# Score products over 64 rows stacked over 128 partitions, and rotated queries transposed two pieces later, in a two-layer encoder kernel

## The chip, the core and the metric

The kernel runs on one core of a Trainium2 chip. The metric is the device time of one execution, in microseconds (us). Before the change it is 834.36 us (median of 3 runs, 832.62 to 834.82).

The core has five engines that work side by side and wait for each other by semaphores: TensorE (PE; its weight loads are shown as PEld) multiplies matrices, VectorE (DVE), ScalarE (ACT) and GpSimd (POOL) work on elements, SyncE (SP) issues the transfers of the weights. TensorE writes to PSUM, and the other operands lie in SBUF; both have 128 partitions ("rows" of an operand below).

## The reference

An encoder trunk of two layers over 256 tokens of 2048 features, in float32. Each layer normalizes x, multiplies it with one wide input matrix, and hands the columns to three attention mixers whose gated results go through an output matrix and are added to x.

```python
for l in range(DEPTH):                      # 2
    h = rmsnorm(x, norm_g[l])
    (a_q, a_k, a_v, a_g, b_cq, b_ckv, b_kr, b_g,
     c_q, c_k, c_v, c_g) = split(h @ w_in[l])
    ya = swa_attention(...)    # A: 8 heads of 128, 2 key/value heads, window, sink
    yb = mla_attention(...)    # B: 4 heads
    yc = diff_attention(...)   # C: 4 heads
    x = x + concat(ya * silu(a_g), yb * silu(b_g), yc * silu(c_g)) @ w_out[l]
return rmsnorm(x, final_norm)

# B, scores of a head: 128 features of its own, and 64 rotated by the position
q_rope = rope(q[..., 128:], positions);  k_r = rope(k_rope, positions)
sc = (q_nope @ k_nope.T + q_rope @ k_r.T) * scale       # k_r is shared by the heads
# C, a head has two softmax maps over 64 features each
sc = (q[:, c] @ k[:, c].T) * scale - slope * dist       # c = 0, 1
attn = softmax(sc[0]) - lam * softmax(sc[1])
```

Two kinds of products run over 64 features: the rotated part of B's scores, and both maps of C.

## The kernel before, in words

*Split products.* A float32 operand x is kept as x = x1 + x2, two parts of 12 bits in the type fp32r. `halves` makes x1 on ScalarE (a copy that rounds) and x2 = x - x1 on VectorE. A full product is three matrix products, x1 y1, x1 y2, x2 y1 (`mm3`, lines 288 to 290).

*Pieces.* All weights come as a list of 266 pieces of up to 512 KB, in the order of use. For each, SP loads it (line 148, four buffers), ScalarE makes its high half `whi` (line 155) and VectorE, in some pieces GpSimd, its low half `wlo` (line 158); both halves have three buffers. The split runs two pieces ahead of the products. `proj_t` (lines 382, 383) uses a piece of four times 128 rows by 256 columns in 16 products; the up-projections of B use theirs in 12 to 24.

*Order.* The program is one long list: a piece's products, then whatever small tasks are due. `later(n, fn)` makes a task due n pieces on, and its first TensorE instruction keeps its place in TensorE's queue. A planner orders the rest within each engine; each engine runs its own queue strictly in order.

*Stacked products.* For 64 features, `stack_q` and `stack_k` put the two parts of an operand into the two halves of the 128 partitions. A pair of products gives the score: [q1; q1] with [k1; k2] over 128 rows (line 431), then q2 with k1 over 64 rows (line 432). `own(c)` is the half of the partitions in which part c lies. The helpers serve three users: `evac_c` (queries and keys of C, out of `proj_t`), `key_transpose` (the rotated key of B), and `finish` in `up_projections` (the rotated queries of B: `use_qr` makes them from a piece, GpSimd rotates them in `rope`, lines 653 to 658, and `finish` transposes them, line 696, three pieces after).

*Users of the scores.* `head_b` has per token tile three full products and one stacked pair, into one PSUM tile. `head_c` has for each map and token tile one stacked pair. The queries' stacked tiles lie in `keep` buffers (the tags yhi and ylo, which the results of the heads take later); `lo64` is a ring of four buffers.

Of the kernel before, what the change touches and what calls it, by code (L numbers as in the profile page):

```python
# [12 lines left out]
F32 = mybir.dt.float32  # L13
F32R = mybir.dt.float32r
# [5 lines left out]
P = 128  # L20
# [10 lines left out]
# 10000 ** (-2 i / 64) in float32  # L31
# [11 lines left out]
def turn_parts():  # L43
    """1 / (2 pi) cut into five parts of 12 bits, the first bit at 2**-3."""
    digits = 0x28BE60DB9391054A7F09D5F47D4D377036D8A5664F10E4107F9458EAF7AEF1586
    bits = 4 * len(f"{digits:x}")
    out, rest = [], digits
    for n in range(5):
        at = bits - 2 - 12 * (n + 1)
        out.append(math.ldexp(rest >> at, at - bits))  # L50
        rest &= (1 << at) - 1
    return out
# [3 lines left out]
def trunk(ctx, tc, x, positions, norm_g, w_in, swa_sink, mla_q_norm, mla_w_uq, mla_kv_norm, mla_w_ukv,  # L56
# [12 lines left out]
    @contextmanager  # L69
    def in_order(*engines, chain=False):  # L70
        """The first instruction that the block traces on each of these engines keeps its place behind
        those traced before it; with chain, all of them do."""
        engines = engines or (nc.tensor,)
        kinds = [e.engine for e in engines]
        traced = nc.cur_bb.bb.instructions
        n = len(traced)
        yield
        for kind in kinds:
            prev = next((i for i in reversed(traced[:n]) if i.engine == kind), None)
            for i in traced[n:]:  # L80
                if i.engine != kind:
                    continue
                if prev is not None:
                    tc.add_manual_dep(i, prev.name, mybir.DependencyInfo(
                        mybir.DependencyClass.NoSync, mybir.DependencyReason.DATA), reason="in_order")
                prev = i
                if not chain:
                    break
# [61 lines left out]
    def split(n):  # L150
        p = pieces[n]
        p["hi"] = wts.tile([P] + p["shape"], F32R, tag="whi", bufs=3, name=f"whi{n}")
        p["lo"] = wts.tile([P] + p["shape"], F32R, tag="wlo", bufs=3, name=f"wlo{n}")
        raw = p.pop("raw")
        nc.scalar.activation(p["hi"], raw, AF.Copy)  # L155
        # GpSimd takes a few of the differences, where VectorE has the attention to do as well
        eng = nc.gpsimd if n > 30 and n % 16 == 15 else nc.vector
        eng.tensor_tensor(p["lo"], raw, p["hi"].bitcast(F32), ALU.subtract)  # L158

    def halves(hi, lo, src, scale=1.0):  # L160
        """hi, lo <- scale * src (SBUF or PSUM) as two parts of 12 bits."""
        nc.scalar.activation(hi, src, AF.Copy, scale=scale)
        if scale == 1.0:
            nc.vector.tensor_tensor(lo, src, hi.bitcast(F32), ALU.subtract)
        else:
            nc.vector.scalar_tensor_tensor(lo, src, scale, hi.bitcast(F32), ALU.mult, ALU.subtract)

# [26 lines left out]
    def rope_constants():  # L194
        H = RD // 2
        # angles in turns, reduced exactly: position * inv is cut into two parts, 1/(2 pi) into five,
        # whose products are exact and lose their whole turns each
# [35 lines left out]
    def distance_constants():  # L233
        # |position - position|, from its upper and lower 16 bits, rounded once
# [17 lines left out]
    def lambdas():  # L252
        # lambda of the differential heads
        pr = work.tile([P, DEPTH, 2, 64], F32, tag="gate", bufs=4, name="lam_pr")
        nc.gpsimd.tensor_tensor(pr, lamp[:, :, :, 0, :], lamp[:, :, :, 1, :], ALU.mult)
        ls = small.tile([P, DEPTH, 2], F32, tag="ls", bufs=1, name="ls")
        later(16, lambda: nc.vector.tensor_reduce(ls, pr, AX.X, ALU.add), nc.vector)
        later(18, lambda: lambda_exp(ls), nc.scalar)
# [6 lines left out]
    def rsqrt(ss, n, w, name, base=None):  # L265
        """(ss / n + eps) ** -0.5 on [P, w]: exp and ln, then a step of Newton's. base: in eps's place."""
# [28 lines left out]
    def later(n, fn, *engines):  # L295
        """fn, n pieces from now; its first instruction on TensorE and on these engines keeps its place."""
        tasks.append((clock[0] + n, fn, engines))
# [10 lines left out]
    def x_stats(L, j, ts=range(NT)):  # L308
        """Sum of squares of one chunk of x, and its transpose times g, in two parts."""
        if not hasattr(L, "ss"):  # L310
            L.ss = small.tile([P, NT, 4], F32, tag="ss_x", bufs=2, name=f"ss{L.l}")
        for t in ts:
            junk = work.tile([P, 512], F32, tag="sb", bufs=3, name=f"sqx{L.l}_{j}_{t}")
            nc.scalar.activation(junk, xc[j][:, t, :], AF.Square, accum_out=L.ss[:, t, j:j + 1])
# [20 lines left out]
    def x_scale(L):  # L335
        """r = rsqrt(mean(x^2) + eps), as a column; x_scale_row: as a row over all partitions."""
        tot = small.tile([P, NT], F32, tag="ss_t", name=f"sst{L.l}")
        nc.vector.tensor_reduce(tot, L.ss, AX.X, ALU.add)
        L.r = rsqrt(tot, D, NT, f"rx{L.l}")
# [11 lines left out]
    def proj_a(L, w, c0, n, nkt, evac):  # L351
        """[token, feature] = h @ w[:, c0:c0+n]."""
# [17 lines left out]
    def proj_t(L, w, c0, evac):  # L370
        """[feature, token] of 256 columns; the two small products share their half of the bank."""
# [19 lines left out]
    def gather(L, f, ps):  # L391
        """f <- the two halves of ps added, times the norm's row."""
# [13 lines left out]
    # Products over 64 rows use both halves of the partitions: [q1; q1] with [k1; k2], and q2 with k1,  # L406
    # where x = x1 + x2. Part c keeps its own rows for x1 of the keys and for x2 of the queries.
# [3 lines left out]
    def stack_q(src, tags, name, scale=1.0):  # L411
        """src(c): the rows of part c. -> {c: [q1; q1]} and q2."""
        top = {}
        lo = work.tile([P, S], F32R, tag="lo64", bufs=4, name=f"lo{name}")
        for c, tag in enumerate(tags):
            t = top[c] = keep.tile([P, S], F32R, tag=tag, name=f"top{name}_{c}")
            for at in (c, 1 - c):
                nc.scalar.activation(t[own(at)], src(c), AF.Copy, scale=scale)
            nc.vector.scalar_tensor_tensor(lo[own(c)], src(c), scale, t[own(c)].bitcast(F32), ALU.mult, ALU.subtract)
        return top, lo  # L420

    def stack_k(src, tiles):
        """src(c): the rows of part c, in their own place. -> {c: [k1; k2]}, k1 in its own place."""
        for c, t in enumerate(tiles):
            nc.scalar.activation(t[own(c)], src(c), AF.Copy)
            nc.vector.tensor_tensor(t[own(1 - c)], src(c), t[own(c)].bitcast(F32), ALU.subtract)
        return dict(enumerate(tiles))

    def mm_stacked(ps, q, k, c, ts, first, last):
        top, lo = q  # L430
        nc.tensor.matmul(ps, top[c][:, ts], k[c], start=first, stop=False)  # L431
        nc.tensor.matmul(ps, lo[own(c), ts], k[c][own(c)], start=False, stop=last)  # L432

    def evac_c(L, dst, i, ps, scale, tag):
# [5 lines left out]
        else:  # L440
            dst[i] = stack_k(src, [keep.tile([P, S], F32R, tag=f"ylo{2 * i + c}", name=f"ck{L.l}_{i}_{c}") for c in range(2)])

    def evac_gate(L, dst, i, ps):
        """silu(g) = g / (1 + exp(-g)) = g exp(min(g, 0) - ln(1 + exp(-|g|)))"""
# [26 lines left out]
    def softmax(S_ps, sb, w, name):  # L471
        """sb[:, :, :w] <- exp(sb - max) in place (from S_ps if given); returns 1 / sum."""
# [67 lines left out]
    def head_b(L, h):  # L540
# [3 lines left out]
        def scores():  # L544
            ps = att.tile([P, NT, S], F32, tag="att", name=f"S{name}")
            (qh, ql), (kh, kl) = L.qb.pop(h), L.kb.pop(h)
            for t in range(NT):
                ts = slice(t * P, (t + 1) * P)
                mm3(ps[:, t, :], qh[:, ts], ql[:, ts], kh, kl, True, False)
                mm_stacked(ps[:, t, :], L.qr[h // 2], L.kr, h % 2, ts, False, True)  # L550
# [17 lines left out]
    def head_c(L, h):  # L568
# [3 lines left out]
        def scores():  # L572
            q, k = L.qc.pop(h), L.kc.pop(h)
            sbs, rrs = [], []
            for c in range(2):
                ps = att.tile([P, NT, S], F32, tag="att", name=f"S{name}_{c}")
                for t in range(NT):
                    mm_stacked(ps[:, t, :], q, k, c, slice(t * P, (t + 1) * P), True, True)
# [67 lines left out]
    def rope(dst, src, t, heads, tmp, name):  # L646
        """dst <- src turned by the angles of its tokens; [P, heads, 64] each."""
# [20 lines left out]
    def key_transpose(L, kt):  # L668
# [3 lines left out]
        L.kr = stack_k(lambda c: ps[own(c)], [work.tile([P, S], F32R, tag=f"kr{c}", bufs=1, name=f"kr{L.l}_{c}") for c in range(2)])  # L672

    def up_projections(L):
# [5 lines left out]
        def use_qr(p):  # L680
# [18 lines left out]
            later(3, finish)  # L699
# [66 lines left out]
    def out_chunk(L, j):  # L766
# [5 lines left out]
        # the columns of each token tile, per bank  # L772
# [53 lines left out]
    def final_add(L, j, t, ps, c):  # L826
        """x += ps in the columns c of chunk j, its sum of squares, and the gain; after the last ones the
        scale and the store."""
# [151 lines left out]
```

## Time and profile before

| | |
|---|---|
| median of 3 runs | 834.36 us |
| span of the profiled execution | 831.4 us; no time of its own is recorded beside it |
| TensorE / VectorE / ScalarE / GpSimd busy | 98 / 71 / 60 / 28% of the span |
| mean busy share of the 16 DMA engines | 58% |
| TensorE's mean granted clock | 0.997 of full speed |

A row of the page's costliest groups, of the list of groups and of one line's instructions names the line, the engine, the operation, what it writes and reads (output <- inputs, buffer numbers left out), the shape, and how often. TensorE's products overlap: a product's duration holds the time in which it passes through the array, while the next one has started. What a product takes of the engine is the distance between two starts.

### The profile page before, as it was taken

What the parts mean: (1) busy time and instruction counts of PE and PEld (TensorE: products, weight loads), DVE (VectorE), ACT (ScalarE), POOL (GpSimd) and SP (SyncE); (2) the same over time, 40 slices, a digit from 0 to 9 for tenths busy, and PEclk for the clock granted to TensorE, in tenths of its full rate; (3) what the DMA queues carried; (4) which work ended last, traced back from release to release, by engine and by line L of the source; (5) the groups of instructions that cost most, each with busy time, mean ns of one, the idle gap of its engine ahead of it and who ended that gap; (6) DMA issues with size and microseconds to landing.
All of it is one profiled execution on the core that took longest, in us unless ns stands there. A gap on an engine that the chain in (4) does not pass through costs nothing. (4 is left out here: it accounts for less than half of the span.)

```text
span 831.4 us, 12804 instructions
## 1 busy us (share of the span) xinstructions
PE 814.6 (98%) x4638; PEld 711.4 (86%) x4638; DVE 587.9 (71%) x951; ACT 495.2 (60%) x942; POOL 230.2 (28%) x266
## 2 busy tenths in 40 slices
PE   8999999999999999999999999999999999999996
PEld 7988888888988888888899888888889888888885
DVE  4767967879768787645556577779787877875554
ACT  5776666667556565554556465757665655664443
POOL 7234232213023444110001243311221432343210
PEclk9999999999999999999999999999999999999998
DMA  8666645464566465556557765464646565557652
GB/s 274 170 194 176 178 130 149 132 176 135 170 177 175 125 180 175 156 178 196 164 158 211 192 169 157 127 176 130 176 127 174 157 177 155 176 152 225 199 183 102
DMA packets 120415, 139.95 MB, mean 168 GB/s; under 512 B 8052, under 2 KB 97728, under 8 KB 120352
## 3 DMA queue, kind: packets, MB, share of 16 engines
q1 hardware_dynamic: 119712, 137.66, 57.2%
q0 software_dynamic: 640, 1.47, 0.6%
q8 instruction: 36, 0.59, 0.3%
q14 instruction: 27, 0.22, 0.1%
HBM read 137.02 MB, written 2.10 MB: 167 GB/s over the span
## 5 line engine op out<-in xcount | busy, mean ns | idle before, releaser
L158 DVE TENSOR_TENSOR wlo<-raw,whi 128x1024 fp32r<-128x1024 f32 (+2 forms) x250 | 297.4, 1194 | 161.7 <-ACT whi L155 160.1
L155 ACT ACTIVATE whi<-raw 128x1024 fp32r<-128x1024 f32 (+2 forms) x266 | 270.8, 1021 | 225.0 <-PE pt L382 78.0
L382 PE MATMUL pt<-h,whi 128*128 128x512 f32 x1088 | 390.0, 400 | 0.0
L383 PE MATMUL pt<-h,wlo 128*128 128x256 f32 x1088 | 305.2, 281 | 1.0 <-DVE wlo L158 1.0
L382 PEld LDWEIGHTS pt<-h,whi 128*128 128x128 f32 x1088 | 204.3, 188 | 46.8
L383 PEld LDWEIGHTS pt<-h,wlo 128*128 128x128 f32 x1088 | 205.6, 189 | 1.6 <-DVE wlo L158 1.6
L288 PE MATMUL po<-whi,yhi 128*128 128x512 f32 (+1 forms) x272 | 103.2, 379 | 0.0
L289 PE MATMUL po<-wlo,yhi 128*128 128x512 f32 (+1 forms) x272 | 102.6, 377 | 0.0
L290 PE MATMUL po<-whi,ylo 128*128 128x512 f32 (+1 forms) x272 | 102.6, 377 | 0.0
L158 POOL TENSOR_TENSOR wlo<-raw,whi 128x1024 fp32r<-128x1024 f32 (+2 forms) x16 | 36.7, 2292 | 188.7 <-ACT whi L155 188.7
L288 PE MATMUL pa<-whi,h 128*128 128x384 f32 (+3 forms) x256 | 85.8, 335 | 0.0
L289 PE MATMUL pa<-wlo,h 128*128 128x384 f32 (+3 forms) x256 | 84.6, 330 | 0.7 <-DVE wlo L158 0.5
L290 PE MATMUL pa<-whi,h 128*128 128x384 f32 (+3 forms) x256 | 84.3, 329 | 0.0
L505 POOL TENSOR_TENSOR ylo<-y,yhi 128x256 fp32r<-128x256 f32 x32 | 35.3, 1104 | 171.8 <-ACT yhi L504 171.7
L290 PEld LDWEIGHTS po<-whi,ylo 128*128 128x128 f32 x272 | 51.2, 188 | 9.5
L288 PEld LDWEIGHTS po<-whi,yhi 128*128 128x128 f32 x272 | 51.2, 188 | 9.1
L289 PEld LDWEIGHTS po<-wlo,yhi 128*128 128x128 f32 x272 | 51.3, 188 | 9.0
L450 POOL TENSOR_SCALAR gm<-g 128x256 f32<-128x256 f32 x32 | 32.7, 1023 | 83.4 <-DVE g L395 83.4
L289 PEld LDWEIGHTS pa<-wlo,h 128*128 128x128 f32 x256 | 48.3, 189 | 4.1 <-DVE wlo L158 1.7
L288 PEld LDWEIGHTS pa<-whi,h 128*128 128x128 f32 x256 | 48.2, 188 | 2.8
L290 PEld LDWEIGHTS pa<-whi,h 128*128 128x128 f32 x256 | 48.2, 188 | 2.5
L454 ACT ACTIVATE ge<-ge 128x256 f32<-128x256 f32 x32 | 13.4, 418 | 34.7 <-POOL ge L453 34.7
(341 smaller groups left out, 1087.6 us busy)
## 6 DMA issues: line engine op xcount, KB each, us to landing
raw<-in_w_in SPq DMA_DIRECT2D x160, 512.0 KB, 3.8
raw<-in_w_out SPq DMA_DIRECT2D x64, 512.0 KB, 4.3
raw<-in_w_in SPq DMA_DIRECT2D x16, 384.0 KB, 3.6
raw<-in_w_in SPq DMA_DIRECT2D x16, 320.0 KB, 3.1
raw<-in_mla_w_uq SPq DMA_DIRECT2D x18, 128.0 KB, 3.0
raw<-in_mla_w_ukv SPq DMA_DIRECT2D x8, 256.0 KB, 3.5
out<-x SPq DMA_DIRECT2D x8, 256.0 KB, 2.8
x<-in_x SPq DMA_DIRECT2D x3, 512.0 KB, 10.2
```

Of the source, the lines that this page charges most:

```text
L155: nc.scalar.activation(p["hi"], raw, AF.Copy)
L158: eng.tensor_tensor(p["lo"], raw, p["hi"].bitcast(F32), ALU.subtract)
L288: nc.tensor.matmul(ps, lhi, rhi, start=first, stop=False)
L289: nc.tensor.matmul(ps, lhi, rlo, start=False, stop=False)
L290: nc.tensor.matmul(ps, llo, rhi, start=False, stop=last)
L382: nc.tensor.matmul(ps, p["hi"][:, kk, fs], L.hh[k], start=k == 0, stop=False)
L383: nc.tensor.matmul(ps[:, S:], p["lo"][:, kk, fs], L.h[k][0], start=False, stop=k == NK - 1)
L450: nc.gpsimd.tensor_scalar(m, g, 0.0, None, ALU.min)
L454: nc.scalar.activation(e, e, AF.Exp)
L505: nc.gpsimd.tensor_tensor(lo, y, hi.bitcast(F32), ALU.subtract)
```

## The change

A query tile now holds both parts of a query, [q1; q2], instead of [q1; q1] and a separate tile for q2. A key becomes two tiles, each with one part on both halves: [k1; k1] and [k2; k2]. A score is then two products over all 128 rows, with the same number of products as before; q2 with k2 is added to what is summed. The rotated key of B comes out of its transpose on both halves already, so that `halves` makes its two tiles. The ring `lo64` holds the second tiles of C's keys, no longer the q2 of the queries. `finish` becomes due five pieces after `use_qr`, not three. The rest of the diff removes comments.

```diff
     def stack_q(src, tags, name, scale=1.0):
         top = {}
-        lo = work.tile([P, S], F32R, tag="lo64", bufs=4, name=f"lo{name}")
         for c, tag in enumerate(tags):
             t = top[c] = keep.tile([P, S], F32R, tag=tag, name=f"top{name}_{c}")
-            for at in (c, 1 - c):
-                nc.scalar.activation(t[own(at)], src(c), AF.Copy, scale=scale)
-            nc.vector.scalar_tensor_tensor(lo[own(c)], src(c), scale, t[own(c)].bitcast(F32), ALU.mult, ALU.subtract)
-        return top, lo
-
-    def stack_k(src, tiles):
-        for c, t in enumerate(tiles):
-            nc.scalar.activation(t[own(c)], src(c), AF.Copy)
-            nc.vector.tensor_tensor(t[own(1 - c)], src(c), t[own(c)].bitcast(F32), ALU.subtract)
-        return dict(enumerate(tiles))
-
-    def mm_stacked(ps, q, k, c, ts, first, last):
-        top, lo = q
-        nc.tensor.matmul(ps, top[c][:, ts], k[c], start=first, stop=False)
-        nc.tensor.matmul(ps, lo[own(c), ts], k[c][own(c)], start=False, stop=last)
+            nc.scalar.activation(t[own(c)], src(c), AF.Copy, scale=scale)
+            nc.vector.scalar_tensor_tensor(t[own(1 - c)], src(c), scale, t[own(c)].bitcast(F32), ALU.mult, ALU.subtract)
+        return top
+
+    def stack_k(src, c, hi, lo):
+        for at in (c, 1 - c):
+            nc.scalar.activation(hi[own(at)], src, AF.Copy)
+            nc.vector.tensor_tensor(lo[own(at)], src, hi[own(c)].bitcast(F32), ALU.subtract)
+        return hi, lo
+
+    def mm_stacked(ps, q, k, ts, first, last):
+        nc.tensor.matmul(ps, q[:, ts], k[0], start=first, stop=False)
+        nc.tensor.matmul(ps, q[:, ts], k[1], start=False, stop=last)
...
-            dst[i] = stack_k(src, [keep.tile([P, S], F32R, tag=f"ylo{2 * i + c}", name=f"ck{L.l}_{i}_{c}") for c in range(2)])
+            dst[i] = [stack_k(src(c), c, keep.tile([P, S], F32R, tag=f"ylo{2 * i + c}", name=f"ckh{L.l}_{i}_{c}"),
+                              work.tile([P, S], F32R, tag="lo64", bufs=4, name=f"ckl{L.l}_{i}_{c}")) for c in range(2)]
...
-                mm_stacked(ps[:, t, :], L.qr[h // 2], L.kr, h % 2, ts, False, True)
+                mm_stacked(ps[:, t, :], L.qr[h // 2][h % 2], L.kr, ts, False, True)
...
-                    mm_stacked(ps[:, t, :], q, k, c, slice(t * P, (t + 1) * P), True, True)
+                    mm_stacked(ps[:, t, :], q[c], k[c], slice(t * P, (t + 1) * P), True, True)
...
-        L.kr = stack_k(lambda c: ps[own(c)], [work.tile([P, S], F32R, tag=f"kr{c}", bufs=1, name=f"kr{L.l}_{c}") for c in range(2)])
+        L.kr = tuple(work.tile([P, S], F32R, tag=f"kr{n}", bufs=1, name=f"kr{n}{L.l}") for n in "hl")
+        halves(*L.kr, ps)
...
-            later(3, finish)
+            later(5, finish)
```

## Rows read from the trace of the kernel before

**Rows 1.** The page, part 1: busy us (share of the span) and instructions.

```profile
PE 814.6 (98%) x4638; PEld 711.4 (86%) x4638; DVE 587.9 (71%) x951; ACT 495.2 (60%) x942; POOL 230.2 (28%) x266
```

**Rows 2.** List of waits of TensorE: us in total, times, longest us.

```profile
PE qrT L696 <- POOL qt L658: 3.3, 2, 1.7
...
PE pt L383 <- DVE wlo L158: 1.0, 1, 1.0
```

**Rows 3.** Timeline of TensorE, scores of the first mixer: start, duration (us), instruction.

```profile
251.74 0.28 PE L289 MATMUL SA<-k_0l,q_0h 128*128 128x256 f32 x1
251.86 0.28 PE L290 MATMUL SA<-k_0h,q_0l 128*128 128x256 f32 x1
```

**Rows 4.** Timeline of TensorE, a head of the third mixer.

```profile
153.37 0.40 PE L382 MATMUL pt<-h,whi 128*128 128x512 f32 x1
153.60 0.28 PE L383 MATMUL pt<-h,wlo 128*128 128x256 f32 x1
153.72 0.28 PE L431 MATMUL SC<-ck,topcq 128*128 128x256 f32 x1
153.93 0.38 PE L432 MATMUL SC<-ck,locq 64*128 64x256 f32 x1
...
156.11 0.50 PE L382 MATMUL pt<-h,whi 128*128 128x512 f32 x1
156.45 0.28 PE L383 MATMUL pt<-h,wlo 128*128 128x256 f32 x1
```

**Rows 5.** Timeline of TensorE, a head of the second mixer.

```profile
96.55 0.28 PE L290 MATMUL SB<-kb_0h,qb_0l 128*128 128x256 f32 x1
96.67 0.28 PE L431 MATMUL SB<-kr,topqr 128*128 128x256 f32 x1
96.88 0.38 PE L432 MATMUL SB<-kr,loqr 64*128 64x256 f32 x1
97.19 0.38 PE L288 MATMUL SB<-kb_0h,qb_0h 128*128 128x256 f32 x1
97.41 0.28 PE L289 MATMUL SB<-kb_0l,qb_0h 128*128 128x256 f32 x1
```

**Rows 6.** Instructions of line 431: duration ns min/median/max, first and last start us.

```profile
L431 PE MATMUL SC<-ck,topcq x32: 278/384/385, 153.7 to 618.6; 128*128 128x256 f32 x32
...
L431 PE MATMUL SB<-kr,topqr x16: 276/278/285, 96.7 to 526.7; 128*128 128x256 f32 x16
```

**Rows 7.** Instructions of lines 418, 419 and 426, the stacked tiles.

```profile
L418 ACT ACTIVATE topcq<-cqf x32: 400/416/420, 130.4 to 578.0; 64x256 fp32r<-64x256 f32 x32
...
L419 DVE SCALAR_TENSOR_TENSOR locq<-cqf,topcq x16: 408/422/2425, 130.8 to 578.3; 64x256 fp32r<-64x256 f32 x16
...
L426 DVE TENSOR_TENSOR ck<-ckf,ck x16: 418/420/422, 144.9 to 597.1; 64x256 fp32r<-64x256 f32 x16
```

**Rows 8.** Timelines of VectorE and TensorE around a key tile.

```profile
146.60 1.22 DVE L158 TENSOR_TENSOR wlo<-raw,whi 128x1024 fp32r<-128x1024 f32 x1
...
150.90 0.40 PE L382 MATMUL pt<-h,whi 128*128 128x512 f32 x1
```

**Rows 9.** Timeline of TensorE, transposes of the rotated queries in both layers; [idle before <- releaser].

```profile
79.02 0.55 PE L696 MATMUL qrT<-ident,qt 128*128 128x128 f32 x3 [1.71 <-POOL qt L658]
...
485.10 0.55 PE L696 MATMUL qrT<-ident,qt 128*128 128x128 f32 x3 [1.56 <-POOL qt L658]
```

**Rows 10.** Timeline of VectorE and TensorE, up-projections of the first layer.

```profile
81.80 2.50 DVE L246 TENSOR_SCALAR dist<-pfrh,pfch 128x256 f32<-128x256 f32 x1
...
89.37 0.39 PE L382 MATMUL pt<-h,whi 128*128 128x512 f32 x1
89.53 1.21 DVE L158 TENSOR_TENSOR wlo<-raw,whi 128x1024 fp32r<-128x1024 f32 x1
```

**Rows 11.** Timelines behind a head of the third mixer.

```profile
163.07 2.35 DVE L158 TENSOR_TENSOR wlo<-raw,whi 128x1024 fp32r<-128x1024 f32 x2
...
164.55 0.60 PE L487 MATMUL PTC<-ident,sbC 128*128 128x128 f32 x4
```

## The prediction

> **What bounds the kernel now.** First the page's busy times: TensorE is busy for 814.6 of the 831.4 us of the span, VectorE for 587.9, ScalarE for 495.2 [rows 1]. With an engine at 98% the question is what it does in that time and where it stands still. Its list of waits answers the second part: 3.3 us in two waits for the rotated queries from GpSimd, and one of 1.0 us for the low half of a weight piece from VectorE, are all it loses in the part of the program that the change touches [rows 2]. For the first part I read its timeline through the score products, by the distance from one start to the next, since the durations overlap. A 128-row product over 256 columns takes 0.12 us of the engine among its like [rows 3]. The score products of the third mixer alternate between 128 rows (line 431) and 64 rows (line 432), and there the distance is 0.21 us once and then 0.31 us at each of them; the first projection product behind them takes 0.34 us to its successor where others take 0.23 [rows 4]. In the second mixer three full products stand before each such pair, and the pair and the product behind it take 0.21, 0.31 and 0.22 us where 0.12 us each would be usual [rows 5]. So the 64-row products are costly both for themselves and for the two full ones around them, and all of that is on the engine that bounds the kernel.
>
> **Part 1: score products over full partitions.** The number of products stays: 32 + 16 of line 431 [rows 6] and as many of line 432, one behind each. What goes is the 64-row form. A head of the third mixer has eight products, from 153.72 to 156.11 = 2.39 us [rows 4]; as full products 8 x 0.12 = 0.96 us, so 1.43 us less, and 0.34 - 0.23 = 0.11 us at the product behind: 1.54 us. Eight heads (four in each of two layers): 12.3 us. In the second mixer each token tile has one pair: 0.21 + 0.31 + 0.22 = 0.74 us [rows 5] become 3 x 0.12 = 0.36 us, 0.38 us less; 8 heads x 2 tiles = 16 times: 6.1 us. Together 18.4 us.
> The stacked form itself is not in the trace. Below, its distance can hardly be under the 0.12 us that the same shape (128 rows, 128 by 256) shows in the first mixer's scores [rows 3]; above, I bound it by 0.21 us, the shortest that line 431 shows before a 64-row product [rows 4, 5]. At 0.21 the 96 products would give back 96 x 0.09 = 8.6 us and the part would be worth 9.8 us. I take 0.12: same shape, same data type, same kind of accumulation.
> Two pages of the Trainium skill disagree on this place. TensorE: Matmul & The Clock Gate, section "Why this matters for your kernels", says that a product over 32 rows takes the time of one over 128; by that the 64-row ones cost nothing extra, and this part would be worth 0 of the 18.4 us. TensorEngine Tiling (Array Packing), section "Key Properties", says that a change of tiling mode drains the engine; by that every passage between the two forms costs, and the sum is the 18.4 us. The trace sides with the second: 0.21, 0.31 and 0.22 us against 0.12 [rows 5], with extra time on the full products at both edges.
>
> **Part 2: the tiles for it.** For the 12 query tiles (8 of the third mixer, 4 rotated) ScalarE's copies go from 4 to 2 each, 24 fewer, VectorE's stay at 2. For the 8 key tiles of the third mixer both go from 2 to 4, 16 more on each. The rotated key goes from two halves each to one tile on both, 2 fewer over the layers. ScalarE: -10 x 0.416 = -4.2 us; VectorE: +14 x 0.42 = +5.9 us [rows 7]. Neither bounds the span, and I cost them at nothing. The cover: per key tile VectorE gets 2 x 0.42 = 0.84 us more. In a layer's first set of keys the low weight half before such a tile's differences ends at 146.60 + 1.22 = 147.82, and the piece that needs it begins at 150.90 [rows 8], so 3.1 us are there. If that cover were gone, the price would be 8 x 0.84 = 6.7 us. The lower bound is 0: VectorE's work elsewhere isn't reduced, and ScalarE's saved 4.2 us lie beside TensorE.
>
> **Part 3: transposes two pieces later.** The step issues no DMA. It is 4 transposes, then 4 copies on ScalarE and 4 differences on VectorE. It moves past a gate piece of 16 products and a query piece of 18, and past whatever the planner puts between on ScalarE, VectorE and GpSimd for the weights; on SP nothing changes. The transposes stand still now for 1.71 us in the first layer and 1.56 us in the second [rows 9], because GpSimd's rotation isn't done. Two pieces are about 5 us of TensorE (8 x 0.35 = 2.8 of the gate piece, 18 x 0.12 = 2.2 of the query piece, by the distances of [rows 3, 4]), more than 1.7, so both waits go. What is late next? The one wait for a low weight half in the list [rows 2] lies in the first layer [rows 10]; the second layer has none, so I take the whole 1.56 us there. In the first layer VectorE makes the distance constants at the same time: one of them takes 2.50 us, and the low half that TensorE waits for at 89.37 is made from 89.53 to 90.74, behind work that had piled up [rows 10]. If VectorE's end there doesn't move, TensorE only arrives earlier and waits longer: gain 0. If the four differences of the moved step no longer stand before it, the gain is up to 1.71 + 1.03 = 2.7 us. If the four come ahead of a low half that has no slack, in either layer, the price is up to 4 x 0.42 = 1.7 us each. In the first layer I take half of 1.71, 0.85 us, since the constants, the piled-up work, are still to be done there. The later end is safe: the transposes then run at about 79.0 + 5 = 84, rotated queries are wanted at 96.67 [rows 5, 9], and a chain of four copies and four differences is 4 x (0.42 + 0.42) = 3.4 us [rows 7].
>
> **The sum.** 12.3 + 6.1 + 1.56 + 0.85 = 20.8 us off the profiled execution's 831.4, so a span of 810.6. Only a span is recorded for that execution; the median of the runs, 834.36, is 2.96 above it, the runs scatter over 2.2 us. 834.4 - 20.8 = 813.6 us.
>
> **Rivals.** *VectorE takes part of it back.* Beside a head of the third mixer VectorE's queue is full. The transposes of its probabilities begin at 164.55; the tile that they read is done at 163.07, when two low weight halves begin which end at 165.42 [rows 11]. So there are 1.5 us of slack, and TensorE gets 1.54 us faster just before. For it: the two sizes are alike. Against it: VectorE's chain starts earlier too, since the scores of the second map come 1.2 us sooner. If half a microsecond comes back at each of the eight heads, and in the first layer part 3 brings nothing, 4 + 0.85 = 4.9 us are lost: 818.5 us.
> *The rows are not the cause.* If a product costs what it does for another reason than its 64 rows, part 1 is worth nothing and the waits alone go: 834.4 - 2.4 = 832.0 us. (TensorE: Matmul & The Clock Gate of the Trainium skill, as read above, would have it so.) For it: the trace has no run of these products in full form. Against it: full products take 0.12 us everywhere else and the cost begins and ends exactly at the 64-row ones [rows 4, 5].
> *Slower: the keys' differences collide with GpSimd.* One difference of the query tiles takes 2.425 us where the median is 0.422 [rows 7], 2.0 more. If all four differences of a key tile did so, VectorE would be 4 x 2.0 + 0.84 = 8.8 us later there, 3.1 of them covered [rows 8]: 5.7 us lost at each of 8 tiles, 46 us against 20.8 gained, 859 us. It decides from 20.8 / 8 = 2.6 us lost per tile, so from the third such difference in a tile on. For it: that one row. Against: the median, and that VectorE's work on key tiles shows 0.42 us in each of 16 cases to within a few ns [rows 7].
>
> **How the numbers follow.** Forecast 0.81, the first rival 0.14, the second 0.03, the third 0.02. Low end of the range: all of both waits and the third goes, 18.4 + 3.3 + 1.0 = 22.7, and 1 us of the runs' scatter: 810.5. High end: the first rival, 818.5. Beyond it lie the other rivals and stacked products that come near 0.21 us (834.4 - 20.8 + 8.6 = 822.2 at that bound), together about a tenth. What a measurement of this kernel can tell from no change is 0.3%, 2.5 us. Faster by more: the first two cases, and half of the second rival, 0.96; within it: 0.02; slower: 0.02 for the third.
>
> **What would show it.** Right: no 64-row form on TensorE; distances of 0.12 us through all score products and 0.23 behind them; a head of the third mixer in 0.96 us; the wait for the rotation gone from TensorE's list. Part 3 shows in the first layer's wait for a low weight half: under 1.9 us and I counted too little, over it too much. Wrong: distances above 0.15 us in the new score products, TensorE waiting for the probabilities or low halves in the third mixer for more than 2 us in all, or VectorE's differences of the keys over 1 us.

## The result and the profile after

Measured: 818.31 us (median of 4 runs, 818.05 to 820.15) beside 834.04 us for the kernel before on the same chip. The ratio is 0.9817, 95% interval 0.9802 to 0.9831; on the 834.36 us shown before that is 819.1 us, 15.3 us less (14.1 to 16.5 by the interval). The forecast was 20.8 us less, 813.6 us, with a range to 818.5. So the direction was right and a quarter of the gain is missing.

The page of the kernel after, its first part: TensorE still bounds the span, VectorE has grown by 4.3 us and ScalarE has 5.3 us less than in [rows 1].

```profile
span 818.3 us, 12804 instructions
...
PE 798.7 (98%) x4638; PEld 707.9 (87%) x4638; DVE 592.2 (72%) x965; ACT 489.9 (60%) x932; POOL 233.3 (29%) x266
```

TensorE's timeline at a head of the third mixer, after (start us, duration, instruction), which answers to [rows 4]: all products have 128 rows, 0.12 us apart, and 0.23 us behind them. The head takes 153.71 - 152.75 = 0.96 us where it took 2.39.

```profile
152.75 0.28 PE L428 MATMUL SC<-ckh,topcq 128*128 128x256 f32 x1
152.87 0.29 PE L429 MATMUL SC<-ckl,topcq 128*128 128x256 f32 x1
...
153.71 0.39 PE L382 MATMUL pt<-h,whi 128*128 128x512 f32 x1
153.94 0.28 PE L383 MATMUL pt<-h,wlo 128*128 128x256 f32 x1
```

The same timeline at a head of the second mixer, which answers to [rows 5]: 0.12 us throughout. Both sizes of part 1 came out as worked out, 1.54 us a head and 0.38 us a pair.

```profile
98.61 0.28 PE L428 MATMUL SB<-krh,topqr 128*128 128x256 f32 x1
98.73 0.28 PE L429 MATMUL SB<-krl,topqr 128*128 128x256 f32 x1
98.85 0.28 PE L288 MATMUL SB<-kb_0h,qb_0h 128*128 128x256 f32 x1
```

TensorE's list of waits, after (us in total, times, longest us), answers to [rows 2]. The wait for GpSimd's rotation and the one for a low half in the first layer are gone. In their place stand two others: 4.0 us for the probabilities of the third mixer, and 2.1 us of a query piece for VectorE.

```profile
PE PTC L485 <- DVE sbC L585: 4.0, 3, 1.4
...
PE pqn L288 <- DVE vb0l L466: 2.1, 1, 2.1
```

Where the time went, in stretches. Each number is the time between the first TensorE products of two pieces in the trace, in us; "both" is an experiment below. Three heads of the third mixer lie in each of its stretches, and one head of the second mixer in each stretch of up-projections.

| stretch | before | after | forecast | both |
|---|---|---|---|---|
| first layer, up-projections | 29.12 | 29.13 | 27.5 | 25.21 |
| first layer, rest of the second mixer | 31.09 | 28.85 | 28.8 | 28.85 |
| first layer, third mixer | 79.95 | 78.80 | 75.3 | 76.81 |
| second layer, up-projections | 27.68 | 25.13 | 25.4 | 25.13 |
| second layer, third mixer | 79.96 | 77.27 | 75.3 | 76.36 |

(Forecast: before, less 1.54 us for a head of the third mixer, 0.76 for one of the second, and 0.85 or 1.56 for the moved transposes.) The missing time lies in the first, third and fifth line. A sixth place has nothing to do with the change: from the first instruction to the ninth weight piece the profiles take 31.00 us before, 32.71 after, and in the experiments 30.4 to 34.2, kernels of both kinds in any order, with TensorE at half clock for a while in some of them and not in others. The profiled execution of the kernel after was 1.7 us slower there than that of before and took 820.15 us; its three other runs took 818.05 to 818.48.

**The first layer's up-projections.** VectorE, GpSimd and TensorE on one timeline, after:

```profile
79.75 0.45 POOL L656 TENSOR_TENSOR qt<-qt,qtmp 128x128 f32<-128x128 f32 x1
80.16 2.36 POOL L158 TENSOR_TENSOR wlo<-raw,whi 128x1024 fp32r<-128x1024 f32 x1
80.23 2.44 DVE L241 CAST pfrl<-pirl 128x256 f32<-128x256 int32 x1 [0.77 <-POOL qt L656]
...
82.66 0.68 DVE L466 TENSOR_TENSOR vb0l<-pvb,vb0h 128x512 fp32r<-128x512 f32 x1
...
83.40 0.39 PE L288 MATMUL pqn<-cTh,whi 128*128 128x256 f32 x1 [2.12 <-DVE vb0l L466]
```

The same conversion, the high half that ScalarE makes for GpSimd's step, and that step, before:

```profile
79.00 0.29 DVE L241 CAST pfrl<-pirl 128x256 f32<-128x256 int32 x1 [0.75 <-POOL qt L658]
80.39 1.06 ACT L155 ACTIVATE whi<-raw 128x1024 fp32r<-128x1024 f32 x1
81.54 2.62 POOL L158 TENSOR_TENSOR wlo<-raw,whi 128x1024 fp32r<-128x1024 f32 x1 [2.57 <-ACT whi L155]
```

After, the conversion at 80.23 has waited for the end of the rotation, and starts just after GpSimd has begun a low weight half. It takes 2.44 us, to within 0.1 us as long as GpSimd's step; the same conversion takes 0.29 us in the kernel before. Behind it in VectorE's queue is the evacuation of a PSUM tile that the next query piece needs, so TensorE stands for 2.12 us. In the kernel before GpSimd's low half began at 81.54: ScalarE stood behind the transposes' wait and made the high half for it only at 80.39; after, it made it at 79.00. Moving the transposes freed ScalarE, GpSimd's step came 1.4 us sooner, and met the conversion. (The Trainium skill, SBUF — State Buffer, section "Terms", says that VectorE and GpSimd arbitrate for one pair of ports and that the loser blocks for the whole instruction; the two durations here agree.)

Behind the wait comes a second price. TensorE's windows, after, show it: the stretch from 84.6 to 87.8 runs at half the clock (1.2 of 2.4 GHz).

```profile
78.00:84.40 6.40, 4.28 (x27) 1.00 0.52 141
84.60:87.80 3.20, 3.20 (x16) 0.50 0.35 125
```

(Columns: stretch, its length, TensorE busy and instructions, granted clock, DMA share, GB/s.) The query piece took 3.87 us there and the next 3.19, where 2.52 and 2.90 are taken without it ("both" below): 1.6 us. Of five traces with this 2.1 us wait, four have the half clock behind it and one ("keypool" below) does not, so the clock's part is real where it shows but does not follow from the wait alone. What parts the one trace from the four is open.

**The third mixer.** The heads whose probabilities come late are one in the first layer, behind another meeting of VectorE and GpSimd, and the third head of each layer. VectorE, GpSimd and TensorE, after:

```profile
176.57 2.38 POOL L158 TENSOR_TENSOR wlo<-raw,whi 128x1024 fp32r<-128x1024 f32 x1 [15.38 <-ACT whi L155]
176.57 3.06 DVE L585 SCALAR_TENSOR_TENSOR sbC<-sbC,rrC,sbC 128x256 f32<-128x256 f32 x2
179.38 0.86 PE L485 MATMUL PTC<-ident,sbC 128*128 128x128 f32 x4 [1.13 <-DVE sbC L585]
...
187.05 3.47 ACT L423 ACTIVATE ckh<-ckf 64x256 fp32r<-64x256 f32 x8
188.32 3.48 DVE L424 TENSOR_TENSOR ckl<-ckf,ckh 64x256 fp32r<-64x256 f32 x8
193.16 0.28 PE L429 MATMUL SC<-ckl,topcq 128*128 128x256 f32 x1
197.14 0.68 DVE L578 SCALAR_TENSOR_TENSOR sbC<-dist,SC 128x512 f32<-128x512 f32 x1
203.59 0.85 PE L485 MATMUL PTC<-ident,sbC 128*128 128x128 f32 x4 [1.45 <-DVE sbC L585]
...
598.99 0.85 PE L485 MATMUL PTC<-ident,sbC 128*128 128x128 f32 x4 [1.38 <-DVE sbC L585]
```

Before, at the same places (the two steps beside the meeting; the last score product of the third head, and the step that takes it up):

```profile
179.84 0.88 DVE L587 SCALAR_TENSOR_TENSOR sbC<-sbC,rrC,sbC 128x256 f32<-128x256 f32 x2
...
196.93 0.38 PE L432 MATMUL SC<-ck,locq 64*128 64x256 f32 x1
197.35 0.69 DVE L580 SCALAR_TENSOR_TENSOR sbC<-dist,SC 128x512 f32<-128x512 f32 x1 [0.30 <-PE SC L432]
```

In the upper three rows two steps that take 0.88 us before take 3.06 us beside GpSimd's 2.38. From 187.05 on, the eight copies and eight differences of the second set's keys end at 190.5 and 191.8, the later 1.4 us ahead of the scores' last product; the step that takes up the second map's scores starts at 197.14, 4 us behind that product. Before, it started 0.4 us behind it. The transposes of this head then wait 1.45 us at 203.59, and 1.38 us in the second layer. A wait costs more than its length: four transposes behind one span 0.85 us, and 0.60 without it ([rows 11]). With that, counted from start to start, the two waits at the third heads cost 3.7 us, and the one behind the meeting 1.5 us.

### The profile page after: what moved, and what is told of

It reads as the page before. It is cut to its first block, busy times and chain, and to the rows that moved or that the text cites. A ratio compares the mean times of both kernels' runs of the same rounds, so it can differ in the third digit from the quotient of the medians.

```text
span 818.3 us, 12804 instructions
## 1 busy us (share of the span) xinstructions
PE 798.7 (98%) x4638; PEld 707.9 (87%) x4638; DVE 592.2 (72%) x965; ACT 489.9 (60%) x932; POOL 233.3 (29%) x266
## 4 chain that ended last, share of the span: by engine, by line
PE 89%; DVE 3%; ACT 3%; POOL 1%; DMA 1%; issue 1%; SPq 0%; ACTq 0%; POOLq 0%
PE pt L382 28%; PE pt L383 14%; PE po L288 7%; PE po L290 7%; PE po L289 7%; PE pa L289 5%; PE pa L290 5%; PE pa L288 5%; DMA x<-in_x 1%; ACT whi L155 1%; DVE wlo L158 1%; PE PTA L485 1%; PE xT L324 1%; PE PTC L485 1%; ACT ckh L423 1%
```

## The experiments

### Is it the rows, or the passage between two forms?

`rows64`, on the kernel before; it leaves out q1 with k2:

```diff
-        nc.tensor.matmul(ps, top[c][:, ts], k[c], start=first, stop=False)
+        nc.tensor.matmul(ps, top[c][own(c), ts], k[c][own(c)], start=first, stop=False)
```

> The kernel before with the first product of each pair over 64 rows too; it leaves out q1 with k2. All 96 score products of the pairs have the 64-row form. Theory A (the passage between the two forms costs about 0.2 us, not the rows): products of a head of the third mixer come 0.12 us apart, but for the passages at both edges and perhaps where the second map goes over to the other half of the rows; a head takes 1.0 to 1.3 us instead of 2.39, the kernel gains 9 to 12 us in the third mixer and 3 us in the second. Rival C (64 rows are slow in themselves): 0.31 us apart throughout, a head takes 2.5 us, the kernel is no faster than before.

Measured: ratio 0.9869 (0.9851 to 0.9887), 10.9 us less. A passage is the step from a product over 128 rows to one over 64, or back. TensorE's timeline:

```profile
155.09 0.28 PE L383 MATMUL pt<-h,wlo 128*128 128x256 f32 x1
155.30 0.40 PE L431 MATMUL SC<-ck,topcq 64*128 64x256 f32 x2
155.53 0.29 PE L432 MATMUL SC<-ck,locq 64*128 64x256 f32 x2
155.64 0.29 PE L431 MATMUL SC<-ck,topcq 64*128 64x256 f32 x2
155.76 0.28 PE L432 MATMUL SC<-ck,locq 64*128 64x256 f32 x2
155.98 0.50 PE L382 MATMUL pt<-h,whi 128*128 128x512 f32 x1
...
97.97 0.28 PE L290 MATMUL SB<-kb_0h,qb_0l 128*128 128x256 f32 x1
98.18 0.38 PE L431 MATMUL SB<-kr,topqr 64*128 64x256 f32 x1
98.41 0.28 PE L432 MATMUL SB<-kr,loqr 64*128 64x256 f32 x1
98.61 0.39 PE L288 MATMUL SB<-kb_0h,qb_0h 128*128 128x256 f32 x1
98.84 0.28 PE L289 MATMUL SB<-kb_0l,qb_0h 128*128 128x256 f32 x1
```

The rows are not slow in themselves: eight products of 64 rows take 0.68 us, even less than eight full ones, and less than the 1.0 to 1.3 us that theory A gave. In the second mixer nothing is gained, 98.84 - 97.97 = 0.87 us where [rows 5] have 0.86. Theory A had expected 3 us there, against its own rule, for the number of passages stays two to a pair. Rival C falls.

`turned`, on the kernel before: the second token tile takes its two products in the other order.

```diff
...
+                    else:
+                        nc.tensor.matmul(ps[:, t, :], q[1][own(c), ts], k[c][own(c)], start=True, stop=False)
+                        nc.tensor.matmul(ps[:, t, :], q[0][c][:, ts], k[c], start=False, stop=True)
```

> The kernel before with the second token tile's pair of the third mixer in the other order: 128, 64, 64, 128 rows, so four passages in a map less two, and the same products. Theory A (a passage costs about 0.2 us): four of the eight passages in a head go, 0.7 to 0.8 us less each, 8 heads, about 6 us less in all, a head takes 1.6 to 1.7 us. Rival C (64 rows are slow in themselves): 2.4 us as before and no gain.

Measured: ratio 0.9921 (0.9903 to 0.9938), 6.6 us less. The same eight products, in the order 128, 64, 64, 128 twice:

```profile
153.67 0.28 PE L431 MATMUL SC<-ck,topcq 128*128 128x256 f32 x1
153.88 0.38 PE L432 MATMUL SC<-ck,locq 64*128 64x256 f32 x1
154.10 0.28 PE L582 MATMUL SC<-ck,locq 64*128 64x256 f32 x1
154.31 0.38 PE L583 MATMUL SC<-ck,topcq 128*128 128x256 f32 x1
...
155.40 0.40 PE L382 MATMUL pt<-h,whi 128*128 128x512 f32 x1
```

The head takes 155.40 - 153.67 = 1.73 us. Over 0.96 us for eight full products that is 0.77 us for four passages, 0.19 us each; in the kernel before 1.54 us for eight, 0.19 us each. Halving the passages halves the cost: part 1 is the passages, and their price is 0.19 us.

### What is the later transposition worth?

`later3`, on the kernel after: `later(5, finish)` back to `later(3, finish)`.

> The changed kernel with the transposes of the rotated queries due after three pieces as before: the stacked products alone. Theory A (the later transposes bring 1.8 us in the second layer and lose 0.7 us in the first): span 0.5 to 1.5 us over the changed kernel's; both waits for GpSimd's rotation are there again, 1.6 to 1.7 us each, and the half clock at 84 us is not. Rival D (the forecast's 2.4 us): 2 to 3 us over it.

Measured: ratio 0.9858 (0.9837 to 0.9879), to be set beside the kernel after, which gave 0.9817 (0.9802 to 0.9831) above and 0.9837 (0.9821 to 0.9853) in `again` below: 3.4 or 1.8 us, too wide to choose. By the stretches, which do not depend on the start: first layer's up-projections 29.37 us against 29.13, second layer's 26.93 against 25.13, so the move brings 0.24 + 1.80 = 2.0 us. That is over what theory A said and at the lower edge of rival D's. Without the move two waits stand where there were [rows 9], and a third:

```profile
PE qrT L695 <- POOL qt L656: 3.1, 2, 1.6
PE pt L383 <- DVE wlo L158: 2.1, 1, 2.1
```

Beside the stacked products alone VectorE's low half in the first layer is late by 2.1 us, not 1.0 as in [rows 2]. So the stacked products by themselves already lose 1.0 us in that stretch: 29.37 us, where 29.12 less the 0.76 of a head would be 28.36.

`only5`, on the kernel before: `later(3, finish)` to `later(5, finish)`.

> The kernel before with the transposes of the rotated queries two pieces later: the move alone. Theory A: the second layer gains 1.6 to 1.8 us, the first layer has the meeting of VectorE and GpSimd as in the changed kernel and loses up to 1 us: 0.7 to 2 us under the kernel before. Rival D: 2.4 us under it. Rival E (the meeting in the first layer comes from the stacked products, not from the move): 3 us under it.

Measured: ratio 0.9973 (0.9962 to 0.9985), 2.3 us less, between A and D and too wide to choose. By the stretches: first layer 29.83 us against 29.12, 0.7 us lost; second layer 25.80 against 27.68, 1.9 us gained; 1.2 us in all. The trace has the same wait and the half clock behind it as the kernel after, with no stacked product in it, so rival E falls:

```profile
81.64 0.39 PE L288 MATMUL pqn<-cTh,whi 128*128 128x256 f32 x1 [2.18 <-DVE vb0l L468]
```

### What happens in the first layer's up-projections?

`again`: the kernel after, unchanged.

> The changed kernel once more, as the base for the next three and to see whether the half-speed clock from 12.8 to 16.2 us and the later start of its profile come back. Theory A (the start of a run varies, the change has no part in it): span about 816.3 as in three of its four runs, the first weight products back at 12.9 us, time 818.1. Rival (the change slows the start): the start is late again, span 818.

Measured: ratio 0.9837 (0.9821 to 0.9853), 819.5 us. The ninth weight piece begins at 31.19 us, near that of before, and the half clock of 12.8 us is not there; the one at 83 us is. So the start varies by itself, as theory A said; its time of 818.1 us did not come back. The stretches are those of the kernel after to 0.3 us.

`dist34`, on the kernel after: VectorE's side of the meeting is moved.

```diff
-    later(26, distance_constants, nc.vector)
+    later(34, distance_constants, nc.vector)
```

> The changed kernel with the distance constants due at piece 34, not 26, so that VectorE doesn't have them while GpSimd makes a low weight half in the first layer's up-projections. Theory A (that meeting makes VectorE late, TensorE waits 2.1 us for a PSUM tile, and its clock drops to half behind the wait): the wait of the query piece and the half clock at 84.5 us go, span 2.5 to 3.5 us under the changed kernel's. Rival B (VectorE is simply too full there, whatever it does): another wait of 1 to 2 us comes in the same stretch, span within 1 us of the changed kernel's.

Measured: ratio 0.9797 (0.978 to 0.9814), 816.45 us, 3.05 us under `again`. The stretch falls from 29.14 to 25.21 us: no wait for the evacuation, no half clock, and no new wait of TensorE in its place. (Its profile's span is not lower by as much, since its start was 3 us later than that of `again`.) This is more than the move of the transposes had cost there: 25.21 us is under the 27.5 that was forecast, since the meeting that the kernel before had in this stretch is gone as well. No run moves the constants in the kernel before.

`skip`, on the kernel after: GpSimd's side is moved, here and behind the head of the third mixer.

```diff
-        eng = nc.gpsimd if n > 30 and n % 16 == 15 else nc.vector
+        eng = nc.gpsimd if n > 30 and n % 16 == 15 and n not in (31, 63) else nc.vector
```

> The changed kernel with two of GpSimd's low weight halves made by VectorE instead, both in the first layer: the one in the up-projections and the one behind the second head of the third mixer. Theory A (a two-operand step of VectorE stands still while GpSimd works on its own two operands): the wait of the query piece (2.1 us) and the half clock behind it go, and so does the wait of 1.1 us for the probabilities of that head; the first layer gains 2 to 4 us, the two waits of 1.4 us at the third head of each layer stay. Rival B (VectorE has too much to do): with 2.4 us more on VectorE both places get later, not earlier.

Measured: ratio 0.9782 (0.9766 to 0.9797), 815.86 us. The first layer's up-projections take 27.20 us instead of 29.13, its third mixer 77.24 instead of 78.80: 3.5 us, with 2.4 us more work on VectorE. Its list of waits:

```profile
PE PTC L485 <- DVE sbC L585: 2.8, 2, 1.4
...
PE pt L383 <- DVE wlo L158: 1.3, 2, 1.0
```

Two of the three waits for probabilities are left, those of the third heads, and the query piece waits no more. Rival B has a share: a wait of 1.0 us for a low half is back, where VectorE has both the constants and the half.

### What makes the probabilities late?

`trans4`, on the kernel after:

```diff
-        later(LAG_T, trans)
+        later(LAG_T + 1, trans)
         later(LAG_V + 1, out_)
```

> The changed kernel with the probabilities of the third mixer transposed four pieces after the scores, not three. Theory A (VectorE finishes them late, TensorE waits for it in three of eight heads, 4.0 us in all, and the transposes behind the waits run slower): the waits of these transposes go, span 4 to 5 us under the changed kernel's. Rival B (VectorE has more to do than TensorE leaves it time for): the wait appears at the next thing that VectorE makes, a low weight half, and the span falls by less than 1.5 us.

Measured: ratio 0.979 (0.9773 to 0.9807), 816.11 us, 3.4 us under `again`. All three waits are gone; the third mixer takes 76.58 and 76.30 us instead of 78.80 and 77.27, which is 3.2 us. Smaller waits take their place for 0.9 + 0.5 us. Theory A's 4 to 5 us were too much, its place was right.

`keypool`, on the kernel after: GpSimd copies the second half of each low key tile.

```diff
-            nc.vector.tensor_tensor(lo[own(at)], src, hi[own(c)].bitcast(F32), ALU.subtract)
+            if at == c:
+                nc.vector.tensor_tensor(lo[own(c)], src, hi[own(c)].bitcast(F32), ALU.subtract)
+            else:
+                nc.gpsimd.tensor_copy(lo[own(at)], lo[own(c)].bitcast(F32))
```

> The changed kernel in which GpSimd copies the second half of each low key tile (16 copies over 64 rows), so that VectorE has the two differences per key tile of the kernel before. Theory A (the doubled work on the key tiles, 1.7 us more on VectorE and 1.7 us more on ScalarE just ahead of the second set's first scores, makes the probabilities late): the waits of 1.4 us at the third head of each layer fall to 0.8 us or less. Rival F (the products alone, which bring TensorE there 1.5 to 3 us sooner, make the wait): they stay at 1.3 to 1.5 us.

Measured: ratio 0.9796 (0.978 to 0.9812), 817.1 us. One wait for probabilities is left, that of the meeting; the two at the third heads are gone altogether. TensorE's list of waits:

```profile
PE PTC L488 <- DVE sbC L588: 1.2, 1, 1.2
PE OB L289 <- DVE ptlB L164: 0.9, 1, 0.9
```

VectorE's timeline at the third head of the first layer, the steps that take up its two maps:

```profile
194.43 1.28 DVE L581 SCALAR_TENSOR_TENSOR sbC<-dist,SC 128x512 f32<-128x512 f32 x2
```

Rival F falls: TensorE comes as soon as in the kernel after, and does not wait. The doubled differences on the keys make these two waits. By which way is open between two: VectorE has 0.84 us less per tile, and the planner now puts the two maps' steps next to each other at 194.43, where it had put the gates between them. No run parts the two. The stretches of the third mixer gain less than the waits: 78.46 us instead of 78.80 and 76.03 instead of 77.27, 1.6 us in all. In the first layer the wait of 0.9 us in the list, ahead of the keys and behind a meeting of VectorE and GpSimd there, stands against it, and in both layers a wait of 0.3 us for a low half comes behind the head.

### Both

> Both moves together. Theory A (two separate places): the gains add, span 6.5 to 8.5 us under the changed kernel's, time about 811, near what was forecast for the change. Rival B: within 2.5 us of the changed kernel's.

`both` has the edits of `dist34` and `trans4`. Measured: 812.49 us (812.17 to 812.77), ratio 0.9749 (0.9735 to 0.9762): 20.9 us under the kernel before and 7.0 us under `again`. The two places add (3.05 + 3.4 = 6.5). It beats both kernels. That it comes to what the forecast had summed, 20.8 us, is luck: by the table `both` is 2.3 us under the forecast in the first layer's up-projections, where the meeting of the kernel before is gone too, and 2.6 us over it in the third mixer. The longest line of TensorE's list of waits among those that the change touches; no other of them is over 0.3 us at once:

```profile
PE OC L289 <- DVE ptlC L164: 0.9, 2, 0.5
```

## Why the prediction was right and wrong

*What bounds the kernel, and part 1: right, in place and size.* The 18.4 us of the score products are all there, 1.54 us a head and 0.38 us a pair. The 0.12 us taken for the stacked form was measured to the hundredth. What the prediction left open, whether rows or passages cost, `turned` and `rows64` settle: passages, at 0.19 us. (By the prediction's own terms the low end of its range would be 810.7, not 810.5; nothing hangs on it.)

*The two pages of the Trainium skill do not disagree.* The prediction set them against each other. TensorE: Matmul & The Clock Gate, section "Why this matters for your kernels", speaks of a product by itself, and `rows64` agrees with it: 64 rows cost no more than 128. TensorEngine Tiling (Array Packing), section "Key Properties", speaks of the change of mode, and `turned` agrees with that. The second rival was thus half true and still gave the wrong time.

*Part 2, "I cost them at nothing": the step that failed, by two waits of 2.8 us, 3.7 us from start to start.* The cover was read at the first set of keys, 3.1 us ahead of a weight half [rows 8]. That is not the place that decides. At the second set, VectorE's doubled differences run just ahead of the scores of the third head, and TensorE waits there for its probabilities 1.45 and 1.38 us; `keypool` takes the doubling from VectorE and both waits go, though its stretches gain only 1.6 us. The sign that the prediction had named for this, waits of more than 2 us for probabilities or low halves in the third mixer, is there: 4.0 us. The prediction named the right consumer, the transposes of the probabilities, in its first rival [rows 11], but tied it to TensorE's speed alone and gave it half a microsecond at every head. That rival's time, 818.5 us, is near what was measured, by other parts: three heads, not eight.

*Part 3 in the second layer: right.* 1.56 us forecast; 1.80 and 1.88 us in the stretches of `later3` and `only5`.

*Part 3 in the first layer, "I take half of 1.71, 0.85 us": wrong in sign.* The stretch gave nothing (29.12 and 29.13 us) although a head of the second mixer in it gained 0.76, so about 0.75 us were lost there against the kernel before, and with the 0.85 us not gained the term is off by 1.6 us. How much of that is the move's depends on what it is added to: alone it loses 0.7 us (`only5`), on top of the stacked products, which by themselves lose 1.0 us, it gains 0.24 (`later3`). The bound below, 0 to -1.7 us, held it, but by another mechanism than the one named. The prediction saw VectorE's 2.50 us step [rows 10] and took it for a long step; it was a meeting with GpSimd, and the question was where the meeting goes when GpSimd's step comes sooner. It went to a step with a PSUM tile's evacuation behind it. `dist34` and `skip` each part the two engines and get 3.9 and 1.9 us back in that stretch.

*The third rival* had the mechanism of that loss (a VectorE step of 2.4 us beside GpSimd) at the wrong place. The keys' differences took 3.48 / 8 = 0.43 us each; the meetings hit the distance constants and, in the third mixer, the weighting of the probabilities, where `skip` gets 1.6 us back.

The sum by its terms, in us, from the stretches: 18.4 for part 1 and about 1.8 for the second layer's transposes as forecast; -0.75 instead of +0.85 in the first layer; -3.5 and -1.9 in the third mixer's stretches, where nothing was charged: 3.7 us of that at the third heads, where `keypool` puts it on part 2's keys, and 1.5 us behind the second meeting, which the prediction had not seen. That is 14.1; the runs say 15.3, between 14.1 and 16.5. (The two profiles differ by 14.8 us behind the ninth weight piece, 0.8 of it in stretches that the change does not touch.)

## What to carry to other kernels

Count passages between product forms, not the rows that a product uses: here each cost 0.19 us on the engine that bounds the kernel, and a passage saved by the order of the products was worth as much as one saved by doing away with a form. When work is added beside the bound, read the cover at each place where it runs, above all at the last one before a consumer, and ask of each step that is moved which engine it sets free and what that engine meets sooner.

## What the runs showed of the hardware that was not expected

Products of 64 rows on the two halves of the partitions run at the same time. In `rows64` the eight products of a head start in four groups of two, 0.01 us apart within a group, and the first stands 0.68 us before the product behind them (the Trainium skill, TensorE: Matmul & The Clock Gate, "Part 3: Packing small matmuls", tells of such overlap between groups of rows; these rows agree). The rows do not name the half that a product uses; that a group holds one product of each map, so one on each half, is inferred. In the second mixer, where a head's products of 64 rows all lie on one half, they start one by one.

A VectorE step that starts while a step of GpSimd runs can stand still for as long as that lasts: 2.44 us beside 2.36 for one of 0.29, and 3.06 us for two of 0.88 beside 2.38. It is not so for every such pair. Where VectorE's low half starts first it takes 1.22 us, as elsewhere ([rows 8]), and GpSimd's step is the one that gets longer, 1.54 us where the same step takes 0.73 at 135.27:

```profile
192.71 1.22 DVE L158 TENSOR_TENSOR wlo<-raw,whi 128x1024 fp32r<-128x1024 f32 x1
192.99 1.54 POOL L503 TENSOR_TENSOR ylo<-y,yhi 128x256 fp32r<-128x256 f32 x1 [14.04 <-ACT yhi L502]
```

TensorE's clock fell to half for 3.4 us behind a single wait of 2.1 us, after two to twelve products at full clock, in four of five traces with that wait.
